# New order numbers for the list scheduler of a two-layer encoder kernel: its product times, its landing times and its table of places

## The chip, the core and the metric

One core of one Trainium2 chip runs the whole program. The metric is device time in microseconds (us) for one execution, taken as the median of several runs; of the kernel before, three runs are known. The engines are named as in the profile: PE is TensorE's matmul side and PEld its weight load, DVE is VectorE, ACT is ScalarE, POOL is GpSimd and SP is SyncE, which here only issues DMAs.

## The reference

An encoder of two layers on 256 tokens (S) of 1024 features (D), in fp32. Cut to what matters:

```python
def mixer_sublayer(x, n1, w_in_l, qg, kg, rpb_l, og, w_out_l, tables):
    h = rms_norm(x, n1)
    proj = h @ w_in_l
    qa, ka, va, qd, kd, vd, qc, kc, vc = jnp.split(proj, cuts, axis=-1)
    out_a = neighbourhood_attention(qa, ka, heads(va, H_NA), rpb_l, na_idx, na_dr, na_dc)
    out_d = dilated_window_attention(qd, kd, heads(vd, H_DIL), dil_idx, dil_val)
    out_c = gqa_block_attention(qc, kc, heads(vc, H_GKV))
    mix = jnp.concatenate([rms_norm(out_a, og[:NA_W]), ...], axis=-1)
    return x + mix @ w_out_l
...
def channel_sublayer(x, n2, w_gu, cw, cb, w_dn):
    h = rms_norm(x, n2)
    g, u = jnp.split(h @ w_gu, 2, axis=-1)
    g = depthwise_conv_centred(g, cw, cb)
    return x + (jax.nn.gelu(g, approximate=False) * u) @ w_dn
...
    for l in range(DEPTH):
        x = mixer_sublayer(x, norm1_g[l], w_in[l], ...)
        x = channel_sublayer(x, norm2_g[l], w_gate_up[l], ...)
```

## The kernel before

**Units of weights.** The weights of a layer are cut into units of 768 KB or 1 MB (`units_of`, L651): first those of `w_in`, in the order dq, dk, dv, cq, ckv, aqk, av, then those of `w_out`, then gate, up and down of the FFN by turns. A unit is loaded from HBM on SP's queue into one of four slots of the tile `raw` (`load`, L688; the trace calls it wp_raw). `split` (L718) then makes two parts of it, chunk by chunk: `hi` is a copy on ACT that rounds to fp32r (a CAST in the trace), `lo` is raw minus hi, a subtraction on DVE. There are two slots each for hi and lo. `mm3` (L752) computes each product as three fp32r products on PE: hi by hi, hi by lo, and lo by hi. The activations are split in the same way when they are turned (act_hT, act_ch and act_cl, act_mixT). Some units of `w_out` and of the second layer are split early and stored to HBM (`keep`, L672: dram_khi and dram_klo, stores on SP's queue), and come back on POOL's queue straight into hi and lo. In the texts, raw4 is the load of unit 4, hi4 and lo4 its parts; units 0 and 1 are of dq, 2 and 3 of dk, 4 and 5 of dv.

**The start.** A list START (L51) issues x in chunks of columns of 128 (two on ACT's queue, three on SP's), the first unit in four pieces w0 to w3, and three rows of gains. PE meanwhile runs 20 products on a constant tile (const_warm, 14 and 6 in the text of the program), whose results nobody reads. x is turned on PE (products with const_ident and const_x), and what comes out is scaled by the gains into act_hT on ACT (hi) and DVE (lo). ACT also squares x for the first norm (ACTIVATE act_s2k<-const_x).

**What sets the order.** Nothing is issued as the program text runs through it. A class `Plan` (L293 to L512) records every operation with what it must wait for; `order()` (L356) then walks a list schedule over all five engines. At each step it takes, of the operations that are ready, the one that can start earliest by its own clock, and among equals the one of lowest rank. The clock comes from `cost()` (L516), from the handover times between engines, and for the first loads from a fixed list:

```python
LANDS = (3400, 3500, 4000, 3600, 5000, 6000, 6800, 7400, 8100, 8900, 8950, 9000)
...
                if i < self.first_loads:
                    end = LANDS[sum(p.method == "dma_start" for p in ops[:i])]
```

The rank is the operation's number in the program text plus a shift plus what the table `PLACES` (L236) holds for that number:

```python
        o.rank = i + self.shift + PLACES.get(i, 0)
...
            for i in self.order():
                o = self.ops[i]
                getattr(o.engine.real, o.method)(*map(real, o.args), **{k: real(v) for k, v in o.kw.items()})
```

So the numbers decide only in which order each engine issues its instructions, and, since slots are given out in that order, which slot of a pool a tile gets. On the chip each engine runs its list in order and waits by semaphores. All instructions are issued from one line, L513, and the rows tell them apart by tile names. Places of the program that the prediction speaks of: the start up to 14.2 us; the products of units 4 and 5 at 25 to 31 us; the stores of khi and klo among the FFN loads of the first layer at 195 to 220 us; and the return of unit 64's parts at 370 to 378 us, a `w_out` unit of the second layer.

Of the kernel before, what the change touches and what calls it, by code (L numbers as in the profile page):

```python
# [57 lines left out]
LANDS = (3400, 3500, 4000, 3600, 5000, 6000, 6800, 7400, 8100, 8900, 8950, 9000)  # L58
# [173 lines left out]
def handover(a, b):  # L232
# [283 lines left out]
def cost(engine, method, args, kw, ins):  # L516
# [9 lines left out]
    n = out.width()  # L526
    psum = any(v.tile.pool.psum for v in ins)
    if engine == "PE":
        if method == "transpose":
            return n / 2.25 + 2.5, 0, 0, "turn"  # L530
        n = args[2].width()
        ns = {512: 231.6, 384: 174.5, 256: 118.0}.get(n, n / 2.25 + 2.5)
        if args[1].dtype == mybir.dt.bfloat16:
            ns = 213.0
# [3 lines left out]
    if engine == "ACT":  # L538
        extra = 88 * sum(isinstance(kw.get(k), View) for k in ("scale", "bias")) + 92 * ("accum_out" in kw)
        ns = 0.833 * n + (53 if psum else 95) + extra  # L540
        return ns, ns + (15 if "accum_out" in kw else 105), 0, None
    if engine == "DVE":
        if method in ("reduce_sum", "reduce_max"):
            n = args[1].width()
# [1043 lines left out]
```

## Time and profile before

| what | value |
|---|---|
| median of 3 runs | 595.62 us (595.15 to 595.68) |
| profiled execution | 595.66 us, of which the span of the profile is 593.6 us |
| PE busy | 588.1 us, 99% of the span, 3424 products and transposes |
| DVE, ACT, POOL busy | 470.9, 412.6 and 77.2 us |
| granted clock of PE | 1.00 in every stretch asked for |
| HBM traffic | 203 GB/s over the span |

The time of the profiled execution and its span differ by 2.06 us that lie around the span. The page's busy time of PE counts pipelined instructions whose ends are modelled, so small losses between two instructions show better as idle time of the weight load (PEld), which can run ahead of a product but waits for the same tiles.

### The profile page before, as it was taken

The numbers are of one execution on the slowest core, as the hardware profiler recorded it, in microseconds if no ns is written. First come the engines' busy times: TensorE is split into PE (matmuls) and PEld (weight loads), VectorE is DVE, ScalarE is ACT, GpSimd is POOL, SyncE is SP. The second block draws the span as 40 slices with busy tenths as digits, with TensorE's granted clock in tenths as the row PEclk, the third lists the DMA queues.
The fourth block names the chain that finished last, engine by engine and source line by source line (L and its number), as shares of the span: only waits on it lengthen the run. The fifth ranks groups of instructions, "written<-read, shape, count | busy, mean of one in ns | idle before, by whom it ended". The sixth has DMA issues, their size and how long they took to land.

```text
span 593.6 us, 9680 instructions
## 1 busy us (share of the span) xinstructions
PE 588.1 (99%) x3424; PEld 508.0 (86%) x3424; DVE 470.9 (79%) x983; ACT 412.6 (70%) x1035; POOL 77.2 (13%) x126
## 2 busy tenths in 40 slices
PE   8999999999999999999999999999999999999997
PEld 6999887888888888888899988778888888888886
DVE  5789889879778998698866897768876777768875
ACT  6789988686564767567686998676765656556661
POOL 1723121150000000000032314421000000000000
PEclk9999999999999999999999999999999999999999
DMA  8893314565599699899554726943554664665701
GB/s 282 302 312 124 116 36 143 181 211 171 203 289 332 217 352 305 294 307 342 176 160 150 260 71 248 348 153 106 168 188 151 208 204 147 213 212 177 238 11 72
DMA packets 85072, 121.37 MB, mean 204 GB/s; under 512 B 9864, under 2 KB 69736, under 8 KB 85024
## 3 DMA queue, kind: packets, MB, share of 16 engines
q1 hardware_dynamic: 82752, 112.10, 56.7%
q0 software_dynamic: 1728, 8.39, 4.0%
q8 instruction: 27, 0.44, 0.3%
q10 hardware_dynamic: 544, 0.26, 0.1%
q14 instruction: 21, 0.17, 0.1%
HBM read 110.86 MB, written 9.88 MB: 203 GB/s over the span
## 4 chain that ended last, share of the span: by engine, by line
PE 97%; ACT 1%; DMA 1%; SPq 0%; issue 0%; DVE 0%; ACTq 0%
PE psw_w L513 51%; PE psa_a L513 46%; DMA const_x<-in_x_dram 1%; ACT act_s2k L513 0%; ACT act_hT L513 0%; ACT wp_hi L513 0%; SPq L513 0%; DVE const_x L513 0%; ACTq L513 0%
## 5 line engine op out<-in xcount | busy, mean ns | idle before, releaser
L513 DVE TENSOR_TENSOR wp_lo<-wp_raw,wp_hi 128x512 fp32r<-128x512 f32 (+2 forms) x332 | 234.2, 734 | 40.7 <-ACT wp_hi L513 26.5
L513 ACT CAST wp_hi<-wp_raw 128x512 fp32r<-128x512 f32 (+2 forms) x332 | 203.8, 668 | 22.4 <-PE psa_a L513 10.4
L513 PE MATMUL psw_w<-act_hT,wp_hi 128*128 128x512 f32 x704 | 182.3, 393 | 0.0
L513 PEld LDWEIGHTS psw_w<-act_hT,wp_hi 128*128 128x128 f32 x704 | 127.7, 188 | 23.5
L513 PE MATMUL psa_a<-wp_hi,act_hT 128*128 128x384 f32 (+2 forms) x448 | 111.9, 332 | 0.4 <-ACT wp_hi L513 0.4
L513 PEld LDWEIGHTS psw_w<-act_hT,wp_lo 128*128 128x128 f32 x704 | 98.1, 188 | 7.8
L513 PE MATMUL psw_w<-act_hT,wp_lo 128*128 128x256 f32 x704 | 102.8, 279 | 0.0
L513 PEld LDWEIGHTS psa_a<-wp_hi,act_hT 128*128 128x128 f32 x448 | 77.8, 189 | 3.5 <-ACT wp_hi L513 0.5
L513 PE MATMUL psa_a<-wp_lo,act_hT 128*128 128x384 f32 (+2 forms) x224 | 74.4, 335 | 0.0
L513 PE MATMUL psa_a<-wp_lo,act_ch 128*128 128x512 f32 (+1 forms) x176 | 68.4, 389 | 0.0
L513 ACT COPY act_s2k<-psw_w 128x256 f32<-128x256 f32 x88 | 32.2, 371 | 50.1 <-PE psw_w L513 49.6
L513 PE MATMUL psa_a<-wp_hi,act_cl 128*128 128x512 f32 (+1 forms) x176 | 66.8, 388 | 0.0
L513 DVE TENSOR_TENSOR act_s2k<-psw_w,act_s2k 128x256 f32<-128x256 f32 x88 | 36.4, 419 | 37.7 <-ACT act_s2k L513 37.4
L513 PE MATMUL psa_a<-wp_hi,act_ch 128*128 128x512 f32 (+1 forms) x176 | 65.9, 388 | 0.0
L513 PEld LDWEIGHTS psa_a<-wp_lo,act_hT 128*128 128x128 f32 x224 | 42.2, 189 | 1.8 <-DVE wp_lo L513 0.3
L513 DVE SCALAR_TENSOR_TENSOR act_s2k<-act_s2k,act_cw,act_s2k 128x255 f32<-128x255 f32 x88 | 37.3, 477 | 1.8 <-ACT act_s2k L513 1.6
L513 PEld LDWEIGHTS psa_a<-wp_hi,act_cl 128*128 128x128 f32 x176 | 33.1, 188 | 6.5
L513 PEld LDWEIGHTS psa_a<-wp_lo,act_ch 128*128 128x128 f32 x176 | 33.1, 188 | 6.3
L513 PEld LDWEIGHTS psa_a<-wp_hi,act_ch 128*128 128x128 f32 x176 | 32.7, 188 | 5.9
L513 ACT ACTIVATE act_s2k<-act_s2k,act_cw 128x256 f32<-128x256 f32 x44 | 24.1, 595 | 19.6 <-DVE act_s2k L513 19.5
L513 POOL TENSOR_TENSOR small_rstd<-small_ms,const_mh 128x6 f32<-128x6 f32 (+2 forms) x26 | 31.9, 1227 | 15.3 <-DVE small_ms L513 13.6
L513 ACT ACTIVATE act_s2k<-act_s2k 128x512 f32<-128x512 f32 x22 | 13.9, 632 | 26.3 <-DVE act_s2k L513 26.3
(131 smaller groups left out, 704.6 us busy)
## 6 DMA issues: line engine op xcount, KB each, us to landing
wp_raw<-in_w_gate_up_dram SPq DMA_DIRECT2D x44, 1024.0 KB, 5.0
wp_raw<-in_w_down_dram SPq DMA_DIRECT2D x22, 1024.0 KB, 5.2
wp_raw<-in_w_in_dram SPq DMA_DIRECT2D x14, 768.0 KB, 4.4
wp_raw<-in_w_in_dram SPq DMA_DIRECT2D x8, 1024.0 KB, 5.3
wp_raw<-in_w_out_dram SPq DMA_DIRECT2D x8, 768.0 KB, 8.3
dram_khi<-act_mixT_hi SPq DMA_DIRECT2D x4, 768.0 KB, 6.1
dram_klo<-act_mixT_lo SPq DMA_DIRECT2D x4, 768.0 KB, 11.4
wp_lo<-dram_klo POOLq DMA_DIRECT2D x4, 768.0 KB, 5.8
```

What stands on the lines that cost most here:

```text
L513: getattr(o.engine.real, o.method)(*map(real, o.args), **{k: real(v) for k, v in o.kw.items()})
```

## The change

Three sets of numbers are replaced. Nothing is added to or taken from the operations; what differs on the chip is the order on each engine and the slots that tiles get.

```diff
-LANDS = (3400, 3500, 4000, 3600, 5000, 6000, 6800, 7400, 8100, 8900, 8950, 9000)
+LANDS = (3600, 3500, 4300, 4100, 5600, 7000, 7200, 7700, 8500, 9300, 9350, 9400)
...
 PLACES = {
-    40: 94, 60: -9, 127: -3, 129: -5, 151: 348, 161: -236, 180: 82, 191: -272, 193: 107, 195: 81, 236: 39, 258: -19,
...
+    76: 291, 82: -188, 123: -22, 139: 110, 157: -5, 158: -5, 159: -5, 161: -5, 169: 63, 171: 63, 175: 303, 200: 253,
...
-        ns = {512: 231.6, 384: 174.5, 256: 118.0}.get(n, n / 2.25 + 2.5)
+        ns = {512: 228.8, 384: 174.2, 256: 118.0}.get(n, n / 2.25 + 2.5)
```

What moves, at three places. A name's number is that of its buffer and can differ between the two kernels; all rows stand at L513 before and at L521 in the changed kernel.

**Place 1, the start.** PE's queue before, from the last of the products on const_warm up to the turning of x's columns 4 to 7 (the rows with const_ident and const_x: the first two turn columns 2 and 3, the last two columns 4 to 7):

```order
L513 MATMUL psa_a_83<-const_warm_77 128x256
L513 MATMUL psa_a_143<-wp_hi_113,act_hT_133 128x384
L513 MATMUL psa_a_143<-wp_lo_121,act_hT_133 128x384
L513 MATMUL psa_a_143<-wp_hi_113,act_hT_133 128x384
L513 MATMUL psa_a_150<-wp_hi_113,act_hT_133 128x384
L513 MATMUL psw_w_156<-const_ident_85,const_x_79 128x128 x2
L513 MATMUL psw_w_116<-const_ident_85,const_x_79 128x128 x2
L513 MATMUL psa_a_143<-wp_hi_113,act_hT_133 128x384
...
L513 MATMUL psa_a_150<-wp_hi_113,act_hT_133 128x384
L513 MATMUL psw_w_119<-const_ident_85,const_x_79 128x128 x4
L513 MATMUL psw_w_124<-const_ident_85,const_x_79 128x128 x4
```

The same place of the changed kernel:

```order
L521 MATMUL psa_a_148<-wp_hi_113,act_hT_135 128x384
L521 MATMUL psa_a_148<-wp_lo_119,act_hT_135 128x384
L521 MATMUL psa_a_143<-wp_hi_113,act_hT_135 128x384 x2
L521 MATMUL psa_a_148<-wp_hi_113,act_hT_135 128x384 x2
L521 MATMUL psa_a_143<-wp_lo_119,act_hT_135 128x384
L521 MATMUL psw_w_165<-const_ident_85,const_x_79 128x128 x2
L521 MATMUL psw_w_121<-const_ident_85,const_x_79 128x128 x2
L521 MATMUL psa_a_143<-wp_hi_113,act_hT_135 128x384
L521 MATMUL psa_a_148<-wp_lo_119,act_hT_135 128x384
L521 MATMUL psa_a_148<-wp_hi_113,act_hT_135 128x384
L521 MATMUL psw_w_125<-const_ident_85,const_x_79 128x128 x4
L521 MATMUL psa_a_143<-wp_hi_113,act_hT_135 128x384
```

Two products stand ahead of the first row shown, so nine products of w0 and w1 stand ahead of the turning of columns 2 and 3, where four stood; between that and the turning of columns 4 and 5 three stand where eight did, and columns 6 and 7 no longer follow at once. Of the 20 products on const_warm, 17 stand ahead of the first transpose where 15 did. ACT's queue in the same stretch, before (the ACTIVATE rows on const_x are the squares, those on psw_w write act_hT, the CAST rows write hi of w2 and w3, then of units 1 and 2):

```order
L513 ACTIVATE act_s2k_163,small_ssx_153<-const_x_79 128x512
L513 CAST wp_hi_113<-wp_raw_81 128x384 x2
L513 ACTIVATE act_hT_133<-psw_w_116,const_gains_130 128x256
L513 ACTIVATE act_hT_133<-psw_w_156,const_gains_130 128x256
L513 ACTIVATE act_hT_133<-psw_w_119,const_gains_130 128x256 x2
L513 ACTIVATE act_s2k_204,small_ssx_153<-const_x_79 128x512
L513 ACTIVATE act_hT_133<-psw_w_124,const_gains_130 128x256 x2
L513 ACTIVATE act_s2k_89,small_ssx_153<-const_x_79 128x512
L513 CAST wp_hi_228<-wp_raw_141 128x384 x4
```

and in the changed kernel:

```order
L521 CAST wp_hi_113<-wp_raw_81 128x384 x2
L521 ACTIVATE act_hT_135<-psw_w_165,const_gains_130 128x256
L521 ACTIVATE act_hT_135<-psw_w_121,const_gains_130 128x256
L521 ACTIVATE act_s2k_196,small_ssx_162<-const_x_79 128x512
L521 ACTIVATE act_hT_135<-psw_w_125,const_gains_130 128x256 x2
L521 ACTIVATE act_hT_135<-psw_w_128,const_gains_130 128x256
L521 ACTIVATE act_s2k_217,small_ssx_162<-const_x_79 128x512
L521 CAST wp_hi_225<-wp_raw_139 128x384
L521 ACTIVATE act_s2k_89,small_ssx_162<-const_x_79 128x512
L521 CAST wp_hi_225<-wp_raw_139 128x384 x3
```

The second square has moved from ahead of the casts of w2 and w3 to behind them, and the last square from ahead of the first cast of unit 1 to behind it.

**Place 2, SP's queue from the small constants to unit 7.** Before (const_dil is the mask of the dilated heads; the three rows of wp_raw behind const_na load units 5 to 7; dram_scr is a store of the neighbourhood table):

```order
L513 DMA act_few_191<-in_rpb_dram 28x1x31
L513 DMA wp_raw_81<-in_w_in_dram 128x4x384
L513 DMA const_dil_206<-in_c_dil_dram 128x2x256
L513 DMA const_na_212<-in_c_na_dram 128x64
L513 DMA wp_raw_141<-in_w_in_dram 128x4x384
L513 DMA wp_raw_158<-in_w_in_dram 128x4x384
L513 DMA wp_raw_166<-in_w_in_dram 128x4x384
L513 DMA wp_raw_81<-in_w_in_dram 128x8x256
L513 DMA dram_scr_445<-act_nab_408 28x1984
```

and in the changed kernel:

```order
L521 DMA act_few_185<-in_rpb_dram 28x1x31
L521 DMA const_dil_193<-in_c_dil_dram 128x2x256
L521 DMA wp_raw_81<-in_w_in_dram 128x4x384
L521 DMA const_na_208<-in_c_na_dram 128x64
L521 DMA wp_raw_139<-in_w_in_dram 128x4x384
L521 DMA wp_raw_153<-in_w_in_dram 128x4x384
L521 DMA dram_scr_351<-act_nab_319 28x1984
L521 DMA wp_raw_159<-in_w_in_dram 128x4x384
L521 DMA wp_raw_81<-in_w_in_dram 128x8x256
```

The load of const_dil now stands ahead of raw4, and the store of the table ahead of raw7 and raw8. On PE the products of raw4 moved too: before, one of them stood ahead of the six transposes of dq, now all 24 do, and of unit 5's two.

**Place 3, the kept parts.** SP's queue before, around the second and third store of dram_khi (the two-word names: in_w_out loads are units to be kept, in_w_gate_up and in_w_down are of the FFN of the first layer):

```order
L513 DMA wp_raw_158<-in_w_gate_up_dram 128x8x256
L513 DMA wp_raw_166<-in_w_out_dram 128x3x512
L513 DMA wp_raw_81<-in_w_gate_up_dram 128x8x256
L513 DMA wp_raw_141<-in_w_down_dram 128x2x1024
L513 DMA dram_khi_2203<-act_mixT_hi_1047 128x1536
L513 DMA wp_raw_166<-in_w_gate_up_dram 128x8x256
L513 DMA dram_klo_2222<-act_mixT_lo_1060 128x1536
L513 DMA wp_raw_158<-in_w_out_dram 128x3x512
L513 DMA wp_raw_141<-in_w_gate_up_dram 128x8x256
L513 DMA wp_raw_81<-in_w_down_dram 128x2x1024
```

and in the changed kernel:

```order
L521 DMA wp_raw_153<-in_w_gate_up_dram 128x8x256
L521 DMA wp_raw_159<-in_w_out_dram 128x3x512
L521 DMA wp_raw_139<-in_w_gate_up_dram 128x8x256
L521 DMA wp_raw_81<-in_w_down_dram 128x2x1024
L521 DMA dram_khi_2225<-act_mixT_hi_1045 128x1536
L521 DMA wp_raw_153<-in_w_gate_up_dram 128x8x256
L521 DMA wp_raw_159<-in_w_out_dram 128x3x512
L521 DMA dram_klo_2263<-act_mixT_lo_1061 128x1536
L521 DMA wp_raw_139<-in_w_gate_up_dram 128x8x256
L521 DMA dram_khi_2344<-act_mixT_hi_1045 128x1536
```

The FFN load behind the store of dram_khi (raw37) takes the slot of the FFN load five rows up (153) instead of that of the kept unit (166 before), and the store of dram_klo has moved behind the load of the next kept unit. When these parts come back, POOL's queue before (act_sqm is a sum of squares of the second layer's mixer):

```order
L513 DMA wp_lo_121<-dram_klo_2222 128x1536
L513 DMA wp_hi_228<-dram_khi_2203 128x1536
L513 TENSOR_TENSOR act_sqm_1081<-act_sqm_1081,act_sqm_1043 128x256
L513 TENSOR_TENSOR small_rstd_504<-small_ms_495,const_mh_101 128x2
L513 DMA act_kc_894<-dram_khi_2620 128x1024
```

and in the changed kernel:

```order
L521 DMA wp_lo_119<-dram_klo_2263 128x1536
L521 TENSOR_TENSOR act_sqm_1078<-act_sqm_1078,act_sqm_1048 128x256
L521 DMA wp_hi_225<-dram_khi_2225 128x1536
L521 DMA act_kc_910<-dram_klo_2686 128x1024
L521 DMA act_kc_896<-dram_khi_2656 128x1024
```

The sum of squares has moved between the two loads, so that unit 64's hi is issued behind it.

## Rows read from the trace of the kernel before

**Rows 1.** The page: its first line, PE's busy time, and the chain's engines.

```profile
span 593.6 us, 9680 instructions
...
PE 588.1 (99%) x3424; PEld 508.0 (86%) x3424; DVE 470.9 (79%) x983; ACT 412.6 (70%) x1035; POOL 77.2 (13%) x126
...
PE 97%; ACT 1%; DMA 1%; SPq 0%; issue 0%; DVE 0%; ACTq 0%
```

**Rows 2.** Waits of PE: who waited for whom, us in total, times, longest.

```profile
PE psa_a L513 <- POOL const_warm L513: 1.0, 1, 1.0
PE psw_w L513 <- DMA const_x<-in_x_dram: 0.5, 1, 0.5
```

**Rows 3.** Busy time of engines by stretch: stretch, its length, PE, PEld, DVE, ACT, POOL.

```profile
125.00:230.00 105.00, 105.00 (x565) 90.56 (x564) 87.81 (x152) 69.31 (x126) 2.46 (x5) 1.00 0.77 259
```

**Rows 4.** Timeline of PEld, start: start, us, instruction, idle before it and releaser.

```profile
5.96 0.30 PEld L513 LDWEIGHTS psa_a<-wp_hi,act_hT 128*128 128x128 f32 x2 [0.22 <-DVE act_hT L513]
7.05 0.42 PEld L513 LDWEIGHTS psw_w<-const_ident,const_x 128*128 128x128 f32 x4 [0.80 <-DMA const_x<-in_x_dram]
...
8.84 0.47 PEld L513 LDWEIGHTS psw_w<-const_ident,const_x 128*128 128x128 f32 x4
9.54 0.42 PEld L513 LDWEIGHTS psw_w<-const_ident,const_x 128*128 128x128 f32 x4 [0.24 <-DMA const_x<-in_x_dram]
...
13.12 0.30 PEld L513 LDWEIGHTS psa_a<-wp_hi,act_hT 128*128 128x128 f32 x2 [0.47 <-ACT wp_hi L513]
13.72 0.19 PEld L513 LDWEIGHTS psa_a<-wp_lo,act_hT 128*128 128x128 f32 x1 [0.30 <-DVE wp_lo L513]
```

**Rows 5.** Timeline of ACT, start.

```profile
6.13 0.51 ACT L513 CAST wp_hi<-wp_raw 128x384 fp32r<-128x384 f32 x1 [0.38 <-DMA wp_raw<-in_w_in_dram]
...
11.94 0.64 ACT L513 ACTIVATE act_s2k<-const_x 128x512 f32<-128x512 f32 x1
...
12.55 1.76 ACT L513 CAST wp_hi<-wp_raw 128x384 fp32r<-128x384 f32 x4
```

**Rows 6.** Timeline of SP's queue: issue of raw4 and of const_dil.

```profile
11.99 0.38 SPq L513 DMA_DIRECT2D wp_raw<-in_w_in_dram  x1
12.42 1.07 SPq L513 DMA_DIRECT2D const_dil<-in_c_dil_dram  x1
```

**Rows 7.** The tile wp_raw, window of raw4's issue alone: issue to landing.

```profile
DMA to landing us min/median/max: 9.8/9.8/9.8
```

**Rows 8.** The tile const_dil: issue to landing.

```profile
DMA to landing us min/median/max: 10.6/10.6/10.6
```

**Rows 9.** Timeline of ACT and of PE: hi4's casts, its first products, dq's transposes.

```profile
21.83 1.76 ACT L513 CAST wp_hi<-wp_raw 128x384 fp32r<-128x384 f32 x4 [0.38 <-DMA wp_raw<-in_w_in_dram]
...
26.21 0.82 PE L513 MATMUL psw_w<-const_ident,act_z 128*128 128x128 f32 x6
```

**Rows 10.** Timeline of POOL: unit 64's loads and the sum of squares.

```profile
370.77 0.54 POOL L513 DMA_DIRECT2D wp_hi<-dram_khi  x1
371.32 0.76 POOL L513 TENSOR_TENSOR act_sqm<-act_sqm,act_sqm 128x256 f32<-128x256 f32 x1
```

**Rows 11.** The tile wp_hi, window of that load's issue alone: issue to landing.

```profile
DMA to landing us min/median/max: 5.8/5.8/5.8
```

**Rows 12.** Timeline of PE: the first product on unit 64's hi.

```profile
378.02 0.48 PE L513 MATMUL psa_a<-wp_hi,act_mixT_hi 128*128 128x512 f32 x1
```

**Rows 13.** Timeline of SP's queue: raw37, and the next kept unit.

```profile
201.99 0.37 SPq L513 DMA_DIRECT2D wp_raw<-in_w_gate_up_dram  x1
...
206.02 0.37 SPq L513 DMA_DIRECT2D wp_raw<-in_w_out_dram  x1
```

**Rows 14.** The tile wp_raw, window of raw37's issue alone: issue to landing.

```profile
DMA to landing us min/median/max: 9.7/9.7/9.7
```

**Rows 15.** Timeline of ACT: raw37's first casts.

```profile
214.56 1.14 ACT L513 CAST wp_hi<-wp_raw 128x512 fp32r<-128x512 f32 x2
```

**Rows 16.** The page's DMA issues: KB each, median us to landing.

```profile
wp_raw<-in_w_gate_up_dram SPq DMA_DIRECT2D x44, 1024.0 KB, 5.0
```

70 rows, old and new, of the table PLACES are left out of this document.

## The prediction

> **What bounds the kernel now.** I read the page first, then the chain of work that ended last, then PE's waits and its busy time by stretch, and last the timelines of the places where the new order differs. The page says that PE is busy for 588.1 of 593.6 us, and 97% of the chain is PE [rows 1]. DVE at 79% and ACT at 70% are fed by PE and feed it, but neither ends the kernel. Of PE's waits the view of waits names one of 1.0 us for the constant that the idle products need at the very start, one of 0.5 us for x, and one more of 0.4 us that the weight load shows below as well [rows 2]. In the long middle PE is busy for 105.00 of 105.00 us [rows 3]. So the reader should see a kernel in which an order can win only what PE still loses, and PE loses it almost only in the first 14 us. There the weight load shows it better than the products do: it waits 0.22 us for act_hT, 0.80 us for x's columns 2 and 3, 0.24 us for columns 6 and 7, 0.47 us for the first hi of unit 1 and 0.30 us for its lo [rows 4], 2.03 us together. Later on I find only losses of 0.1 to 0.2 us between single products, about 1 us over the whole middle as I estimate it from start-to-start times. The 1.0 us ahead of the first idle product and the last store behind the last product are the same in both orders. What there is to win is therefore about 3 us, 0.5% of the time; what there is to lose has no such ceiling.
>
> **What the new numbers do by themselves.** Nothing. The 228.8 and 174.2 ns and the new LANDS are only the planner's clock, and no instruction gets longer or shorter. PE's products are the same 3424 in number and shape, and each engine issues what it issued. I cost this at 0. All that follows is order, and the sum is made on the profiled execution's 595.66 us, 0.04 us above the median.
>
> **Place 1, the start.** Two more idle products stand ahead of the first transpose. Idle products at that point take some 0.1 to 0.2 us each, so I let everything behind them start 0.2 us later: +0.2. The wait of 0.22 us for act_hT stood ahead of the third product [rows 4]; now products of the other token tile stand there, and I take it as gone: -0.2. Nine products instead of four now stand ahead of the turning of columns 2 and 3. These products fill the 0.80 us in which PE waited for x [rows 4]: -0.8. But the last three of the nine need w1, whose cast on ACT ran from 6.13 to 6.64 [rows 5]; lo comes about 0.6 us behind hi, as 13.12 and 13.72 show for unit 1 [rows 4], so at about 7.2. By products of about 0.17 us PE gets there at about 6.9: +0.35. What is late next is x's columns 4 and 5. Their turning began at 8.84 without a wait [rows 4], with eight products ahead of it; now three are, so PE arrives earlier than the data can have been there for certain. I take +0.3 (0 if they had long landed, 0.5 if they landed just at 8.8). Columns 6 and 7 no longer follow at once, so their 0.24 us goes: -0.25.
>
> On ACT the last square, 0.6 us of queue from 11.94 to 12.55 [rows 5], now stands behind the first cast of unit 1 instead of ahead of it. That cast is what PE waited 0.47 us for; the load had landed by then, so I take half of it away: -0.2. The second cast of unit 1 still stands behind both squares, so lo's wait of 0.30 us stays or grows: +0.1. The other square, put behind the casts of w2 and w3, only delays what POOL makes of the squares, which PE needs far later: 0. The place sums to +0.2 - 0.2 - 0.8 + 0.35 + 0.3 - 0.25 - 0.2 + 0.1 = **-0.5 us**. Its lower bound is that all replaced waits stay away (-1.2), its upper that the new waits eat all of it (0).
>
> **Place 2, the mask ahead of raw4.** Before, raw4 was issued at 11.99 and landed 9.8 us later, at 21.8; the mask was issued at 12.42 and landed 10.6 us later, at 23.0 [rows 6 to 8]. They landed in the order of their issue, 1.2 us apart, with 256 KB in the second. With the mask ahead I let raw4 land at 23.0. Then its first cast, which began at 21.83 [rows 9], begins at about 23.1, is done after 0.44 us (four take 1.76), and lo is there 0.6 us later, at about 24.1. PE's first product on it stood right ahead of dq's transposes at 26.21 [rows 9], so at 26.0; with half a microsecond won at the start it comes at 25.5. That leaves 1.4 us: the swap itself costs 0. The cover is thin, though: all 24 products of unit 4 now follow at once (24 by about 0.17 us, some 4.2 us), where 6 transposes and other products were mixed in, so hi5 is wanted at about 29.7. The casts of unit 5 now stand on ACT between scalings of dk (act_z), which wait for POOL's power. No row shows that wait; I take **+0.2 us**. Below, 0; above, 1.5, which is raw4 or raw5 later by 1.2 us more and one cast (0.44 us) that is no longer covered. The store of the table, now ahead of raw7 and raw8, belongs in the same bounds.
>
> Here the Trainium skill bears on the argument: "DMA: Bandwidth & Descriptors", section "Queues, rings and completion order", says that each DMA engine takes the descriptors of one row in ring order, but that completion is not in order of issue for an issuing engine. By its second half raw4 need not land later at all. By the row the two landed in order and 1.2 us apart; the swap costs 0 by either, but by the page the 0.2 us for what follows would go as well, and the sum below would be 595.5.
>
> **Place 3, the kept parts.** When unit 64 comes back, its hi was issued at 370.77 and landed 5.8 us later, at 376.6 [rows 10, 11]; the first product on it started at 378.02 [rows 12]. Now the sum of squares, 0.76 us on POOL [rows 10], stands ahead of the issue: landing at up to 377.3. At the same time the product moves ahead of three of the four transposes behind which it stood, 0.4 us, and PE is some 0.3 us ahead by then: it is wanted at about 377.0 to 377.3. I take **+0.3 us**, with 0 (the sum of squares is late or early enough not to matter) and 0.7 (the whole of it) as ends.
>
> The stores of khi and klo I cost at 0. raw37 was issued at 201.99 and landed 9.7 us later, at 211.7 [rows 13, 14], and ACT first cast it at 214.56 [rows 15]: 2.9 us of cover. In the new order it takes the slot that the next kept unit had, and that was free only at 206.02 [rows 13]. So it is issued about 4 us later, but behind less of the store of khi. With the 5.0 us that such loads take in the median [rows 16] it lands at 211 to 213, in time. With the old 9.7 us it does not; that is the first rival.
>
> **The sum.** 595.66 - 0.5 + 0.2 + 0.3 = 595.66; the other places where rows trade places, by my reading each under 0.2 us either way, I take as 0. Against the median this is 595.6 us, no change that a measurement of this kernel can tell (about 0.2%, 1.2 us).
>
> **The rivals.**
> *Slower, by raw37.* If the load behind the store of khi still takes 9.7 us when it is issued at 206 to 208, it lands at 215.7 to 217.7. The cast that came at 214.56 is then up to 3.1 us late, less the 0.5 us by which ACT ran ahead of PE: PE waits about 2.6 us at 217, and the time is about 598.2. It decides when the landing is past 214.5. For it speaks that loads in this stretch took twice the median [rows 14, 16]; against it, that the store of klo has moved behind and no longer shares the wires with it.
> *Slower, by raw4.* If raw4 lands at 24.3 rather than 23.0, or the casts of unit 5 stand behind scalings that wait for POOL, PE waits up to 1.5 us between 25 and 31 us: about 597.1.
> *Faster.* If w1's lo is in time and columns 4 and 5 had landed long before 8.84, place 1 gives -1.2; with no wait at place 2 and 3 and 0.3 us of the small losses in the middle gone, the time is about 594.1. Against it: every product moved ahead of one late load stands ahead of another load that was itself not early [rows 4].
> *The order does nothing.* PE is full in both, the waits only change their names at the start, and nothing new waits later: 595.3 to 595.7.
>
> **How the numbers follow.** The likeliest is the sum, in which small gains and losses cancel: 0.50, with its own range 595.0 to 596.5. That the order does nothing: 0.20. Faster: 0.12, all of it below the 0.2%. raw37: 0.10, raw4: 0.08, both slower by more than 0.2%. So faster 0.12, the same 0.70, slower 0.18. The range reaches down over the upper part of the faster case, to 594.4, and up over raw4's case, to 597.3; raw37's case stays out, and with the rest of the faster one this leaves under 2 in 10 outside.
>
> **What would show it.** Place 1 is right if the weight load's wait of 0.80 us for const_x is gone, a wait for wp_hi or wp_lo of 0.3 to 0.4 us stands near 7 us and one for const_x near 8.8 us, and unit 1's first product comes about 0.5 us earlier against its place in the order. Place 2 is right if raw4 lands near 23.0 and PE shows no wait for wp_hi over 0.3 us between 25 and 31 us. Place 3 is right if PE shows 0 to 0.7 us at about 377 us that ends with dram_khi, and none at 205 to 220 us. The prediction is wrong if PE's busy share falls in a stretch of the middle that was full before, or if PE's work between 14 and 580 us itself gets shorter, which I hold to be fixed.

## The result, and the profile after

The changed kernel takes 597.43 us (median of 7 runs, 596.87 to 598.30) against 595.62 us (595.15 to 595.98): 1.0032 times the time before, 95% interval 1.0023 to 1.0041. It is slower by 0.3%; the forecast was no change, with 597.3 us as the upper end. The span grew from 593.6 to 595.6 us in the profiled executions.

The page of the changed kernel, the same lines as in [rows 1]:

```profile
span 595.6 us, 9692 instructions
...
PE 589.8 (99%) x3424; PEld 508.8 (85%) x3424; DVE 469.6 (79%) x983; ACT 411.6 (69%) x1035; POOL 79.0 (13%) x126
...
PE 95%; ACT 2%; POOL 2%; DVE 1%; issue 0%; POOLq 0%
```

PE's share of the chain fell from 97 to 95%, and POOL, which was not in that line before, is in it with 2%, some 12 us. The page counts PE busy at 99% in both, which hides the loss. So I took the start-to-start time of every two neighbouring instructions of PE in both traces, set it against the usual time of its kind, and added up what is over by stretch. Up to 14.2 us the changed kernel has 0.3 us less of it than before, from there to 36 us 1.1 us more, to 290 us 0.1 us less, from 290 to 335 us 1.3 us more, and behind that as much as before: 2.0 us in all, which is the difference of the spans. The medians of the device times differ by a little less, 1.8 us. Most of both losses lies where the projections of dv and cq run, once in each layer.

The timeline of the weight load (PEld) of the changed kernel, where it waited: the start, units 4 and 5 of the first layer, and the same units of the second, 54 to 58.

```profile
13.32 0.19 PEld L521 LDWEIGHTS psa_a<-wp_lo,act_hT 128*128 128x128 f32 x1 [0.52 <-DVE wp_lo L521]
...
26.96 0.19 PEld L521 LDWEIGHTS psa_a<-wp_lo,act_hT 128*128 128x128 f32 x1 [0.32 <-DVE wp_lo L521]
30.68 0.30 PEld L521 LDWEIGHTS psa_a<-wp_hi,act_hT 128*128 128x128 f32 x2 [0.80 <-ACT wp_hi L521]
...
318.10 0.19 PEld L521 LDWEIGHTS psa_a<-wp_hi,act_hT 128*128 128x128 f32 x1 [0.36 <-DVE act_z L521]
...
330.92 0.48 PEld L521 LDWEIGHTS psa_a<-wp_hi,act_hT 128*128 128x128 f32 x3 [0.78 <-ACT wp_hi L521]
```

The waits for const_x of [rows 4] are gone, as are the one for act_hT and the one for unit 1's hi. In their place stand waits for hi and lo. On PE itself the product at 30.68 is late by 0.64 us and the one behind it by 0.11, and at 330.91 it is 0.63 and 0.11; the two places cost 1.5 us together. The smaller waits are late by less on PE: 0.28 us at 26.96 and 0.31 at 318.10.

The chain of waits of the changed kernel from 24 to 32 us (start, length, what) says where the first of them comes from:

```profile
22.68 2.82 POOL small_rstd L521 x2
25.51 0.55 POOL act_sdk L521
26.06 0.36 POOL const_gq L521
26.42 0.09 issue
26.52 0.93 POOL small_ms L521
27.45 0.07 issue
27.52 1.55 POOL small_rstd L521
29.07 0.02 issue
29.09 1.13 ACT act_z L521 x5
30.23 0.41 ACT wp_hi L521
30.64 0.04 issue
30.68 0.62 PE psa_a L521 x2
```

It is read from the bottom: the product at 30.68 waits for a cast (wp_hi), which stands in ACT's queue behind five scalings of dk (act_z), which wait for the power of the norm (small_rstd), which POOL does behind five other things. Two of POOL's steps are also longer here than they are elsewhere in these traces: small_ms took 0.93 us and the power 1.55, where the shortest of their kind take 0.28 and 1.32 (the last section comes back to this). ACT itself has time: its timeline shows it idle while the cast, whose load had long landed, stands behind the scalings.

```profile
27.37 0.59 ACT L521 CAST wp_hi<-wp_raw 128x384 fp32r<-128x384 f32 x1
29.09 1.13 ACT L521 ACTIVATE act_z<-psa_a,small_rstd 128x64 f32<-128x64 f32 x5 [1.14 <-POOL small_rstd L521]
30.09 0.53 ACT L521 CAST wp_hi<-wp_raw 128x384 fp32r<-128x384 f32 x1
...
328.86 1.14 ACT L521 ACTIVATE act_z<-psa_a,small_rstd 128x64 f32<-128x64 f32 x5 [1.32 <-POOL small_rstd L521]
329.86 0.61 ACT L521 ACTIVATE const_v<-psa_a,small_rx 128x384 f32<-128x384 f32 x1
330.32 0.95 ACT L521 CAST wp_hi<-wp_raw 128x384 fp32r<-128x384 f32 x2
```

The third row is the chunk of hi5 that PE wants first, cast third; in the second layer the last row is the first chunk of hi58. ACT stood idle for 1.14 and 1.32 us ahead of the scalings. In the kernel before the same engine had no such place in the first layer. Its timeline:

```profile
26.45 0.50 ACT L513 CAST wp_hi<-wp_raw 128x384 fp32r<-128x384 f32 x1
...
33.07 1.14 ACT L513 ACTIVATE act_z<-psa_a,small_rstd 128x64 f32<-128x64 f32 x5 [0.62 <-POOL small_rstd L513]
```

There the wanted chunk of hi5 was cast at 26.45 and the scalings came at 33.07, behind the casts of hi5 and three of hi6. In its second layer the scalings came at 328.36, and PE waited not for a cast but ahead of its transposes of dq (and, 0.14 and 0.06 us late, ahead of those of dk at 333.08):

```profile
315.62 0.31 PEld L513 LDWEIGHTS psw_w<-const_ident,act_z 128*128 128x128 f32 x3 [0.20 <-DVE act_z L513]
...
328.36 1.14 ACT L513 ACTIVATE act_z<-psa_a,small_rstd 128x64 f32<-128x64 f32 x5 [0.54 <-POOL small_rstd L513]
```

### The profile page after: what moved, and what is told of

Its sections match the earlier page's. It is cut to its first block, busy times and chain, and to the rows that moved or that the text cites. A ratio compares the mean times of both kernels' runs of the same rounds, so it can differ in the third digit from the quotient of the medians.

```text
span 595.6 us, 9692 instructions
## 1 busy us (share of the span) xinstructions
PE 589.8 (99%) x3424; PEld 508.8 (85%) x3424; DVE 469.6 (79%) x983; ACT 411.6 (69%) x1035; POOL 79.0 (13%) x126
## 4 chain that ended last, share of the span: by engine, by line
PE 95%; ACT 2%; POOL 2%; DVE 1%; issue 0%; POOLq 0%
PE psw_w L521 51%; PE psa_a L521 44%; POOL small_rstd L521 1%; ACT act_s2k L521 1%; POOL small_ms L521 1%; ACT act_z L521 0%; DVE wp_lo L521 0%; ACT wp_hi L521 0%; ACT const_v L521 0%; POOL act_sdk L521 0%; DVE const_x L521 0%; ACT act_qo L521 0%; DVE act_qo L521 0%; POOL const_gq L521 0%; DVE act_sw L521 0%
## 5 line engine op out<-in xcount | busy, mean ns | idle before, releaser
L521 DVE TENSOR_TENSOR wp_lo<-wp_raw,wp_hi 128x512 fp32r<-128x512 f32 (+2 forms) x332 | 233.3, 734 | 56.7 <-ACT wp_hi L521 41.8
L521 ACT CAST wp_hi<-wp_raw 128x512 fp32r<-128x512 f32 (+2 forms) x332 | 202.2, 666 | 23.5 <-PE psw_w L521 12.6
L521 PE MATMUL psw_w<-act_hT,wp_hi 128*128 128x512 f32 x704 | 181.3, 393 | 0.0
L521 PEld LDWEIGHTS psw_w<-act_hT,wp_hi 128*128 128x128 f32 x704 | 127.2, 188 | 23.4
L521 PE MATMUL psa_a<-wp_hi,act_hT 128*128 128x384 f32 (+2 forms) x448 | 112.8, 334 | 1.0 <-ACT wp_hi L521 0.9
L521 PEld LDWEIGHTS psw_w<-act_hT,wp_lo 128*128 128x128 f32 x704 | 98.6, 188 | 8.3
L521 PE MATMUL psw_w<-act_hT,wp_lo 128*128 128x256 f32 x704 | 103.6, 280 | 0.0
L521 PEld LDWEIGHTS psa_a<-wp_hi,act_hT 128*128 128x128 f32 x448 | 78.1, 189 | 5.3 <-ACT wp_hi L521 1.8
L521 PE MATMUL psa_a<-wp_lo,act_hT 128*128 128x384 f32 (+2 forms) x224 | 74.1, 335 | 0.2 <-DVE wp_lo L521 0.2
L521 PE MATMUL psa_a<-wp_lo,act_ch 128*128 128x512 f32 (+1 forms) x176 | 68.2, 389 | 0.0
L521 PE MATMUL psa_a<-wp_hi,act_cl 128*128 128x512 f32 (+1 forms) x176 | 66.9, 388 | 0.0
L521 PE MATMUL psa_a<-wp_hi,act_ch 128*128 128x512 f32 (+1 forms) x176 | 66.2, 389 | 0.0
L521 ACT COPY act_s2k<-psw_w 128x256 f32<-128x256 f32 x88 | 32.0, 371 | 46.1 <-PE psw_w L521 45.9
L521 DVE TENSOR_TENSOR act_s2k<-psw_w,act_s2k 128x256 f32<-128x256 f32 x88 | 36.2, 420 | 28.9 <-ACT act_s2k L521 28.4
L521 PEld LDWEIGHTS psa_a<-wp_lo,act_hT 128*128 128x128 f32 x224 | 42.3, 189 | 2.0 <-DVE wp_lo L521 0.8
L521 PEld LDWEIGHTS psa_a<-wp_hi,act_cl 128*128 128x128 f32 x176 | 33.1, 188 | 6.4
L521 PEld LDWEIGHTS psa_a<-wp_lo,act_ch 128*128 128x128 f32 x176 | 33.1, 188 | 6.0
L521 PEld LDWEIGHTS psa_a<-wp_hi,act_ch 128*128 128x128 f32 x176 | 32.9, 188 | 6.2 <-ACT act_ch L521 0.3
L521 ACT ACTIVATE act_s2k<-act_s2k,act_cw 128x256 f32<-128x256 f32 x44 | 24.1, 596 | 19.9 <-DVE act_s2k L521 19.7
L521 DVE SCALAR_TENSOR_TENSOR act_s2k<-act_s2k,act_cw,act_s2k 128x255 f32<-128x255 f32 x88 | 37.1, 479 | 0.8 <-ACT act_s2k L521 0.7
L521 ACT ACTIVATE act_s2k<-act_s2k 128x512 f32<-128x512 f32 x22 | 13.9, 633 | 29.1 <-DVE act_s2k L521 29.1
L521 POOL TENSOR_TENSOR small_rstd<-small_ms,const_mh 128x6 f32<-128x6 f32 (+2 forms) x26 | 31.9, 1229 | 13.4 <-DVE small_ms L521 11.9
```

## The experiments

Eight kernels take the changed kernel's list and put single operations elsewhere in it, by this edit and a line of pairs (the operation, and the one ahead of which it now stands); four exchange the planner's numbers:

```diff
+        order = self.order()
+        for i, ahead_of in MOVES:
+            order.remove(i)
+            order.insert(order.index(ahead_of), i)
         with self.tc.manual_schedule():
-            for i in self.order():
+            for i in order:
```

All times are medians beside runs of the kernel before on the same chip; the ratio is to that kernel. The 597.43 us of the changed kernel were taken beside other runs of it, so kernels are better set side by side by their ratios (the changed kernel's is 1.0032, 1.0023 to 1.0041). Differences of 0.2 to 0.5 us between two of them lie within the intervals; what a single move does is read from the trace, and the time bears it out only where intervals stand apart, as they do for the fifth experiment here and the last.

**The cast of hi5 first.**

```diff
+MOVES = ((300, 267), (301, 186),)
```

> The changed kernel with two operations moved in the list and nothing else: the cast of the first chunk of hi5 stands ahead of the first scaling of dk (act_z) on ACT, and its lo ahead of the second token tile's rotation on DVE. Queue theory (the changed kernel loses its time where casts stand on ACT behind scalings that wait for POOL's power): the wait of PE at 30.68 us (0.64 us, and 0.11 us on the product behind it) is gone, the time falls by 0.75 us to about 596.7. Landing theory (the loads of units 4 and 5 are late): no change at 30.7 us, 597.4. Start theory (the time is lost in the first 14 us, by the clock): 597.4.

597.20 us (1.0029, 1.0018 to 1.0040): 0.2 us less than the changed kernel, not 0.75, though the interval reaches to the 0.75. Its weight load's waits:

```profile
27.19 0.19 PEld L528 LDWEIGHTS psa_a<-wp_lo,act_hT 128*128 128x128 f32 x1 [0.46 <-DVE wp_lo L528]
...
34.25 0.30 PEld L528 LDWEIGHTS psa_a<-wp_hi,act_hT 128*128 128x128 f32 x2 [0.70 <-ACT wp_hi L528]
```

The wait at 30.68 is gone, as the queue theory said and the two others did not. But one of the same kind and size stands at 34.25, for hi6: its cast is queued behind the scalings of dk's second token tile, which wait for the next power. The mechanism held, the price did not: in the trace a place in a queue was mended, and the next one behind it took over.

**The cast of hi58 first.**

```diff
+MOVES = ((3124, 3035),)
```

> The changed kernel with one operation moved: the cast of the first chunk of unit 58's hi (cq of the second layer) stands ahead of the scalings of dk of that layer on ACT. Queue theory: PE's wait at 330.91 us (0.63 us and 0.11 us behind it) is gone, the time falls by about 0.74 us to 596.7, and what stands before 330 us stays as it is. Landing theory and start theory: no change, 597.4.

596.89 us (1.0022, 1.0014 to 1.0031), 0.5 us less. In its trace the wait at 330.9 is gone and the wait at 30.66 is there as before. From 330 to 340 us the weight load has one wait, 0.31 us for act_z at 333.84, which the changed kernel's trace does not have; PE is late by 0.15 and 0.06 us there. So here too a wait follows, a smaller one: 0.74 less 0.21 is 0.53.

**Six waits at once.**

```diff
+MOVES = ((300, 267), (301, 186), (3124, 3035), (229, 185), (2938, 2928), (3831, 3581), (83, 156),)
```

> The changed kernel with both casts moved ahead of their scalings, and with four more single operations moved: the last chunk but one of lo4 ahead of a scaling of dq on DVE (wait at 26.96 us), a scaling of dq of the second layer earlier on DVE (wait at 318.09 us), unit 64's hi issued ahead of the sum of squares on POOL (379.62 us), the first lo of unit 1 ahead of the copy of the gains on DVE (13.31 us). Queue theory: every one of these waits is a place in a queue, the sum is 0.75 + 0.74 + 0.28 + 0.3 + 0.33 + 0.4 = 2.8 us, of which I take 2.5 as some come back later: 594.9, under the kernel before. If the waits only move to the next late thing (rival): not under 596.5.

596.60 us (1.0019, 1.0010 to 1.0028): 0.8 us less, where I took 2.5. That is just above the 596.5 at which I would have called the rival right, and in this size the rival is half right. Its interval still touches the changed kernel's. The waits at 30.7, 330.9 and 379.6 us are gone. Those for lo shrank, from 0.52 to 0.29 us for unit 1 and from 0.32 to 0.28 for unit 4 (weight load; the same wait is 0.46 in three profiles with fewer moves, so the last step is no gain); the one at 318 stayed, since the earlier scaling only made the next one late (0.32 us on PE at 317.54); and hi6 waits as in the first experiment, 0.72 us on the weight load at 33.20.

**raw4 ahead of the mask again.**

```diff
+MOVES = ((122, 295),)
```

> The changed kernel with raw4 issued ahead of the mask of the dilated heads again, as before, and nothing else. Queue theory: hi4 is cast about 0.3 us earlier, which nothing waits for, 597.4, no change within 0.2 us. Landing theory (the mask ahead of raw4 is what made the products of units 4 and 5 wait): the waits at 26.96 and 30.68 us shrink, about 596.4.

597.40 us (1.0030, 1.0018 to 1.0041): no change. Its first cast of hi4 began at 21.85, as before the change, and PE waits at 27.08 and 30.79 as it did without the edit. So in the median the swap of the two loads costs nothing that can be measured.

**hi6 too.**

```diff
+MOVES = (..., (343, 285),)
```

> The kernel of all seven moves, and one more: the first cast of hi6 (cq of the first layer) ahead of the scalings of dk's second token tile on ACT. Queue theory, mended (a cast moved past one set of scalings leaves the next cast behind the next set, since both sets wait for POOL's powers one after the other): the wait at 33.20 us of that kernel (0.57 us and 0.11 behind it) goes, 0.68 us less, about 595.9. If the wait only moves on to hi6's later chunks or to lo6: no change, 596.6.

596.25 us (1.0012, 1.0003 to 1.0021), 0.35 us less than the kernel of seven moves. The wait at 33.20 is gone, without a successor, and the interval lies below the changed kernel's. The profiled execution was the slowest of its eleven (597.98 us). PE, ACT and DVE in it, then POOL, and the same operation of POOL in the changed kernel's profile:

```profile
23.74 1.75 ACT L528 CAST wp_hi<-wp_raw 128x384 fp32r<-128x384 f32 x4 [1.67 <-DMA wp_raw<-in_w_in_dram]
...
25.50 0.56 DVE L528 TENSOR_TENSOR act_z<-psa_a,small_rstd 128x384 f32<-128x384 f32 x1 [2.57 <-POOL small_rstd L528]
...
26.20 0.42 PE L528 MATMUL psa_a<-wp_hi,act_hT 128*128 128x384 f32 x1 [0.67 <-DVE act_z L528]
```

```profile
20.34 1.18 DVE L528 COPY act_nab<-act_few 28x1984 f32<-28x1984 f32 x1 [2.51 <-DMA act_few<-in_rpb_dram]
20.39 2.87 POOL L528 TENSOR_TENSOR act_cdk<-const_rot,const_gk 128x128 f32<-128x128 f32 x1
...
21.45 1.48 DVE L528 TENSOR_TENSOR wp_lo<-wp_raw,wp_hi 128x384 fp32r<-128x384 f32 x3
```

```profile
20.53 0.46 POOL L521 TENSOR_TENSOR act_cdk<-const_rot,const_gk 128x128 f32<-128x128 f32 x1
```

The four casts of hi4 began 1.3 us later than in the changed kernel's profile, where they began at 22.43. Of this, 0.8 us is a later issue of raw4 (12.80 instead of 12.01), and the landing took 10.8 instead of 10.3 us. But the casts were done at 25.5, and PE's product at 26.20 did not wait for them. It waited for DVE's scaling of dq, which frees the tile that the product writes and which waited 2.57 us for POOL's power. POOL was late by an operation that took 2.87 us in place of 0.46, beside the copy and three subtractions of DVE. So the cover that the prediction worked out for raw4 held in this execution too, and what it lost at this point came by way of POOL's power again.

**15 idle products ahead of the first transpose.**

```diff
+MOVES = ((18, 20), (19, 20),)
```

> The changed kernel with two of its 17 idle products moved back behind the first transposes of x, so that 15 stand ahead of them as before; nothing else. Start theory: at the pace that PE has there (0.21 us from one idle product to the next) the first product on x comes 0.4 us earlier, and nothing at the start hides it: 0.4 us less, 597.0. Queue theory: the start was gained from, not lost; 0.2 us or less, and the waits at 26.96, 30.68 and 330.91 us stay.

597.11 us (1.0033, 1.0020 to 1.0046). The median is 0.3 us less than 597.43, the ratio is not lower than the changed kernel's, and the interval holds both expectations: no gain is shown. The timelines of PE show why this is hard to tell; first the changed kernel's, then that of the kernel with seven moves, whose PE does the same up to this point:

```profile
4.94 1.12 PE L521 MATMUL psw_w<-const_ident,const_x 128*128 128x128 f32 x4
5.85 0.85 PE L521 MATMUL psa_a<-const_warm 128*128 128x256 bf16 x3
6.35 0.67 PE L521 MATMUL psa_a<-wp_hi,act_hT 128*128 128x384 f32 x1
```

```profile
4.82 0.65 PE L528 MATMUL psw_w<-const_ident,const_x 128*128 128x128 f32 x4
5.32 0.49 PE L528 MATMUL psa_a<-const_warm 128*128 128x256 bf16 x3
5.82 0.44 PE L528 MATMUL psa_a<-wp_hi,act_hT 128*128 128x384 f32 x1
```

The same four transposes take 0.91 us from their start to the next row in one and 0.50 in the other: they follow each other at 0.21 us at first and at 0.11 later on. The moment from which PE works at twice the pace differs from one execution to the next, and with it the first product on x: 6.35 here, 5.82 there, 6.18 in this experiment. Among profiles in which the pace doubled early, the first product comes at 5.44 and 5.39 with 15 idle products ahead (the kernel before and the last experiment) and at 5.82 and 5.94 with 17, which puts the price of the two at 0.4 to 0.5 us there.

**The numbers without the table, the table without the numbers.** Two more kernels cross the change; the first is the kernel before with

```diff
-LANDS = (3400, 3500, 4000, 3600, 5000, 6000, 6800, 7400, 8100, 8900, 8950, 9000)
+LANDS = (3600, 3500, 4300, 4100, 5600, 7000, 7200, 7700, 8500, 9300, 9350, 9400)
...
-        ns = {512: 231.6, 384: 174.5, 256: 118.0}.get(n, n / 2.25 + 2.5)
+        ns = {512: 228.8, 384: 174.2, 256: 118.0}.get(n, n / 2.25 + 2.5)
```

and the second is the changed kernel with the same two edits the other way round.

> The kernel before with the new LANDS and product times, but its old table PLACES. 673 of PE's 3360 operations stand elsewhere than before, 2692 elsewhere than in the changed kernel. If the new times make the planner's clock truer and that is what counts: not slower than before, 595.6 or less. If a table of offsets is fitted to the clock it was made with, and loses its fit with another: slower, by the waits that single casts and loads get, 596.5 to 598.

603.65 us (1.0138, 1.0125 to 1.0152), worse than the upper end of either expectation.

> The changed kernel with the old LANDS and product times, so the new table PLACES alone. 2853 of PE's 3360 operations stand elsewhere than before. If the table alone brings the loss: the same as the changed kernel, 597.4, with its waits at 26.96, 30.68 and 330.91 us. If table and times belong together: slower than the changed kernel, 598 or more.

618.14 us (1.0378, 1.0364 to 1.0392). The waits of PE in the first, and one stretch and one wait of PEld in the second:

```profile
PE psa_a L513 <- ACT wp_hi L513: 3.1, 5, 1.6
PE psw_w L513 <- ACT act_s2k L513: 1.1, 2, 0.8
```

```profile
50.00:125.00 75.00, 66.51 (x421) 52.55 (x421) 57.16 (x161) 54.25 (x156) 12.90 (x18) 0.93 0.24 79
```

```profile
58.77 0.28 PEld L521 LDWEIGHTS psa_a<-wp_hi,act_hT 128*128 128x128 f32 x1 [5.00 <-ACT wp_hi L521]
```

The largest part that has a name is again casts that come too late, 3.1 of the 8.2 us in the first kernel; most of the rest I did not trace, in the second kernel above all. In the second PE loses 8.5 of 75 us in that stretch, and its granted clock there is 0.93 in the mean: behind an idle time of 5 us PE was not at its full level of 2.4 GHz throughout. Either half of the change without the other costs far more than both together; the table is fitted to the very numbers with which the planner's clock runs.

**LANDS alone, the product times alone**, each an edit of one of the two lines above in the kernel before.

> The kernel before with the new LANDS alone (old product times, old table). 269 of PE's 3360 operations stand elsewhere, 216 of them among the first 300. Theory of the fit (a table of offsets holds only with the clock it was made with): the waits of the kernel with both new numbers that lie before about 60 us come back, 1.8 us at 25.02 us the largest, some 4.5 us: about 600, and nothing after 100 us. Rival (LANDS nearer to the landings gives a better start): 595.4 or less.

600.33 us (1.0078, 1.0061 to 1.0095).

> The kernel before with the new product times alone (old LANDS, old table). 552 of PE's 3360 operations stand elsewhere, 10 of them among the first 300. Theory of the fit: the other part of the loss of the kernel with both, at 60 to 130 us and 370 to 400 us, some 3.5 us: about 599, with a start like that of the kernel before. Rival (1% on the time of a product is too little to matter): 595.6.

600.42 us (1.0085, 1.0070 to 1.0100). Both lose, as the theory of the fit had it: 4.6 us where it said 4.5, and 4.7 where it said 3.5, so the second was mis-sized by 1.2. A difference of 1.2% in the planner's time of one product shape and of 0.2% in another's moves 552 of PE's operations and costs 4.7 us.

**POOL's power earlier.**

```diff
+MOVES = ((258, 283), (455, 283),)
```

> The changed kernel with two POOL operations moved and nothing else: the preparation of sdk (0.58 us) and the scaling of the query gains (0.39 us) stand behind the power of dk's first token tile instead of ahead of it. If the casts wait for POOL's power as its queue gives it: that power comes 0.5 us earlier, PE's wait at 30.68 us falls from 0.64 to about 0.15 us and the time by 0.5 us, to 596.9; the wait at 330.91 us stays. If only the casts' place on ACT counts and POOL is not late: no change, 597.4.

597.21 us (1.0026, 1.0015 to 1.0037), 0.2 us less. The power came 1.6 us earlier, at 27.49 instead of 29.05, and the wait at 30.68 is gone entirely. I had expected 0.5 us: the two operations put behind it had taken 0.9 us, and at the earlier time small_ms took 0.35 instead of 0.93 us and the power 1.32 instead of 1.55. So a part of the 1.6 us is POOL's own speed. But the power of the second token tile came no earlier, and hi6 waits behind it:

```profile
33.97 0.30 PEld L528 LDWEIGHTS psa_a<-wp_hi,act_hT 128*128 128x128 f32 x2 [0.85 <-ACT wp_hi L528]
```

This is the first experiment's result by another way: whichever end of the first link is loosened, the next one holds. In time, 0.2 us is not told from nothing.

**All of it.**

```diff
+MOVES = ((300, 267), (301, 186), (3124, 3035), (229, 185), (3831, 3581), (83, 156), (343, 285),
+         (122, 295), (258, 283), (455, 283), (18, 20), (19, 20),)
```

> The changed kernel with all that the runs so far pointed at: the casts of hi5, hi6 and hi58 ahead of scalings of dk, the lo of units 1 and 4 earlier on DVE, unit 64's hi ahead of the sum of squares, 15 idle products ahead of the first transpose, raw4 ahead of the mask, and on POOL the power of dk's first token tile ahead of two preparations that nothing waits for yet. Queue theory: every place where PE still lost more than 0.3 us in one of those runs has cover again, about 595.4, level with the kernel before (within 0.2%). If the loss lies in PE's own order: not under 596.2, where the kernel with eight moves stands.

595.97 us beside 595.70: 1.0006, 0.9998 to 1.0015, level with the kernel before. In its profile the waits of PE are

```profile
PE psa_a L528 <- POOL const_warm L528: 1.0, 1, 1.0
PE psa_a L528 <- ACT wp_hi L528: 0.3, 1, 0.3
PE psw_w L528 <- DMA const_x<-in_x_dram: 0.3, 1, 0.3
```

all three in the first 10 us. Twelve moves of single operations, two of them idle products and none a product on weights, give back what the change lost as far as the interval can tell, which runs from 0.1 us less to 0.9 us more than before. Not every small wait is gone: the move of operation 2938 of the third experiment is left out, the wait at 318 stays (0.31 us on PE), and by start-to-start times this profile still has some 0.5 us more than the kernel before from 14.2 to 36 us and 0.7 from 290 to 335 us, against 0.5 less at the start. So the loss can be mended by places in the queues of ACT, DVE, POOL and SP, and the order of PE's products on weights need not be touched for it. PE's new order still has a part in when each cast is wanted; no run puts PE's products back and leaves the other queues as they are.

## Why the prediction was wrong, point by point

**What bounds the kernel** held: PE does, and what an order can change is what PE loses at single places.

**The numbers by themselves** cost nothing on the chip, as written. What the prediction did not see is how hard they decide: alone they cost 8.2 us, and the new table alone 22.7.

**Place 1**, forecast -0.5 us, came out at -0.3, but not by its terms. The wait for x at 7 us went, unit 1's first wait went, and its lo's grew from 0.30 to 0.52 us on the weight load (I had 0.40). The +0.35 for w1's lo near 7 us and the +0.3 for columns 4 and 5 did not come: PE was later there than I had it, and reached the columns only at 9.26. The two idle products were mis-sized: I took +0.2, and the first product on x came at 6.35 instead of 5.44. Of these 0.9 us, 0.4 to 0.5 is the price of the two products by the profiles named above, and the rest goes with the later pace, which differs between executions of one order. That the sum of the place came near is luck.

**Place 2** named the right mechanism and gave it too small a size. The swap itself cost nothing in the median, as forecast: raw4 landed at 22.3 and not near 23.0, and raw4 alone put back gave 597.40. The +0.2 us for the casts between the scalings became 0.75, inside its bounds of 0 to 1.5, with 0.3 more for a lo behind a scaling on DVE at 26.96: 1.05 in all. The sign given for this place, no wait for wp_hi over 0.3 us between 25 and 31 us, failed at 30.68. What came is the second condition of the rival "slower, by raw4", casts of unit 5 behind scalings that wait for POOL, which had 0.08 and 597.1 us.

**Place 3** came out as written: unit 64's hi was issued at 373.06 and landed 6.5 us later, at 379.6, where the product on it started at 379.62, 0.22 us late and 0.11 on the next: 0.33 where 0.3 was forecast. Behind 335 us as a whole the changed kernel loses no more than before, so this was made up elsewhere in that stretch.

```profile
379.62 0.19 PEld L521 LDWEIGHTS psa_a<-wp_hi,act_mixT_hi 128*128 128x128 f32 x1
```

The rival of raw37 didn't come about: issued at 207.19, inside the 206 to 208 given, it landed after 5.1 us, and PE waited for nothing there.

**The step that failed** is two terms of the sum: the +0.2 of place 2, which measured 1.05, and the half sentence that takes the other places as 0, "by my reading each under 0.2 us either way". That one measured 0.7. The second layer has the same units, the same scalings behind the same power, and there the order had put one product of unit 58 ahead of unit 57's last: 0.74 us at 330.91 and 0.31 at 318.09, where the kernel before lost 0.35 at its transposes of dq and dk. I had found the mechanism at 30 us, said that no row showed its wait, and not looked for its second place. With 1.05 in the place of 0.2, and 0.7 for the second layer, the sum is 595.66 - 0.3 + 1.05 + 0.3 + 0.7 = 597.4, the median measured. That it meets the median so well is partly luck: it counts the 0.3 of place 3, which was made up behind 335 us, and leaves out what the stretch from 290 to 335 us lost beyond the 0.7, some 0.6 us. Of that, 0.2 us is two products near 327.5 that came 0.11 us late each, the first behind a hi; the rest I did not trace. That the waits at 30.68 and 330.92 come from a place in a queue and not from a load is shown by the moves of one cast each, after which they are gone from the traces; that such moves are enough for the time, by the kernel with all of them. How much of the lateness of POOL's power is its queue, and how much that POOL itself was slow, no run separates.

The Trainium skill enters here as it did in the prediction: "DMA: Bandwidth & Descriptors", section "Queues, rings and completion order", allows a later load to complete first. The traces here show none among the loads of SP's queue whose landing they give: the mask, issued ahead at 11.49, landed after 8.9 us at 20.4, raw4, issued at 12.01, after 10.3 us at 22.3; with raw4 ahead it was the other way round.

## What to carry to other kernels

Where an engine works its queue in order, ask of each operation that feeds the bound engine not how long it takes but what stands ahead of it and what that waits for; a short cast behind a scaling that waits for another engine's slow power is as late as the power. Mend such a place together with the next one behind it, since here the wait moved on along the queue; and when one layer shows it, look for the same place in every layer. A table of offsets that was fitted to a planner's clock can be worse than useless with another clock (8.2 and 22.7 us here): make the numbers truer only together with a new fit, and judge the two as one.

## What the runs showed of the hardware that I had not expected

The same instruction can take three times as long on POOL, and in these traces it does so only beside certain work of DVE. POOL's and DVE's timelines of the changed kernel, the same operation on the same shape for the two token tiles:

```profile
321.75 0.28 POOL L521 TENSOR_SCALAR small_ms<-small_ss,small_he 128x6 f32<-128x6 f32 x1 [5.12 <-ACT act_s2k L521]
...
326.34 0.90 POOL L521 TENSOR_SCALAR small_ms<-small_ss,small_he 128x6 f32<-128x6 f32 x1 [2.50 <-DVE act_sw L521]
```

```profile
322.09 0.56 DVE L521 TENSOR_TENSOR wp_lo<-wp_raw,wp_hi 128x384 fp32r<-128x384 f32 x1 [1.83 <-ACT wp_hi L521]
...
326.15 0.55 DVE L521 TENSOR_TENSOR wp_lo<-wp_raw,wp_hi 128x384 fp32r<-128x384 f32 x1
326.62 0.55 DVE L521 TENSOR_TENSOR act_z<-act_z,act_cdk 128x384 f32<-128x384 f32 x1
```

DVE was idle ahead of 322.09, so the first ran alone; the second ran beside operations of DVE with two inputs in SBUF. The Trainium skill's "GPSIMD Engine Reference", section "1. Specifications", says that POOL's way to SBUF is shared with VectorE and contended when DVE has two inputs in SBUF. These rows agree, and so do all 14 profiles: of the 168 operations small_ms on 128x6, the 73 that overlap no DVE operation of this kind (two inputs in SBUF, or a copy within it) took 0.27 to 0.29 us each, and the 95 that overlap one took 0.27 to 1.06. No run here takes DVE's work away to show the cause. It bears on the argument: the small_ms and the power ahead of the wait at 30.68 took 0.93 and 1.55 us where 0.28 and 1.32 are the shortest, 0.9 us together, where PE lost 0.75 us.

The start of PE is not the same from one execution to the next: with one and the same order the transposes of x took 0.91 or 0.50 us, though the granted clock reads 1.00 in both. The runs of the kernel before lie within 0.8 us (595.15 to 595.98), those of the changed one within 1.4, and those of the kernel with all moves, whose median is level, within 2.6 (595.28 to 597.86). Whether an order whose covers are just long enough scatters more is not shown.
